# Attention units in turns of two, later ends of heads, and early output weights in a hybrid decoder layer

## The chip, the cores and the metric

The kernel runs on one core of a Trainium2 chip. The metric is the device time of one execution in microseconds (us); the lower, the better. The engines are named as in the profile: PE multiplies matrices (PEld loads its weights), DVE is the vector engine, ACT the activation engine, POOL the general one, SP issues most transfers. SBUF is the memory on the chip that all engines read, PSUM the eight banks into which PE writes its results.

## What is computed

One layer of a decoder for 1024 tokens of width 2048, in float32. The input is normalized, one projection (2048 to 6656 columns) gives eight groups, two kinds of attention follow, their outputs are normalized and gated, and an output projection (2048 by 2048) with another norm is added to the input. Cut to what matters here:

```python
q_sb, k_sb, v_sb, z_sb, q_sw, k_sw, v_sw, z_sw = split(einsum(rmsnorm(h), w_in))
# stick-breaking, 16 heads of 64, over all earlier keys
z = q_sb @ k_sb * scale
w = exp(log_sigmoid(z) + suffix_sum(log_sigmoid(-z)))      # only s < t
o_sb = w @ v_sb
# sliding window of 128, 16 heads on 4 key groups, with bias and a sink logit
p = softmax_with_sink(q_sw @ k_sw * scale + bias)
o_sw = p @ v_sw
o = concat(rmsnorm(o_sb) * silu(z_sb), rmsnorm(o_sw) * silu(z_sw))
h = h + rmsnorm(o @ w_out)
```

## The kernel before

**Projection.** The 6656 columns are 52 blocks of 128. A block is one call of `proj` (line 477): for each of 16 slices of the inner dimension and each of two halves of the tokens, three matmuls of 128x128 by 128x512 (high and low parts of both operands, since one float32r product is not exact enough). Weights come in four groups `kg` of four slices: `split_w` (line 128) loads a group into `wraw` by SP, ACT copies its high part (`whi`, line 133) and DVE subtracts the low part (`wlo`, line 135). After each slice and half, that is after every three matmuls, `step` (line 276) calls `advance`.

**Attention units.** Between those matmuls the attention is done in units, in the order in which `offer` queued them. A stick-breaking unit (`unit_sb`, line 535) is 256 rows by 256 keys of one head, 160 units in all, in 8 pairs of heads named sb0 to sb7; a unit sb3_0_1_2 is pair 3, head 0, row block 1, key block 2. A sliding-window unit (`unit_sw`, line 609) is 128 rows by 256 keys of two heads; there are 64, in groups sw0 to sw3. Each unit has three steps on PE, with work of other engines between them:

- `s1`: four score matmuls into `z` (PSUM tag pz, two banks). Then, for stick-breaking, two sigmoids on ACT (`m`, `b`: lines 555 and 557), two running products on DVE (lines 565, 568; a unit goes on from the `m` of the one before it in its row) and a product on DVE (line 571); on the diagonal a mask on POOL (line 561) comes before that. For the sliding window, a maximum, exponentials and a scaling on DVE and ACT (lines 639 to 654).
- `s2`: three or four transposes of the result into `wt` (PSUM tag pw, two banks); ACT copies the high part `wh`, DVE subtracts the low part `wl` (lines 586, 587 and 665, 666).
- `s3`: four output matmuls of `wh` and `wl` with the values `v` into `o` (PSUM tag po, **one** bank). Units of one row block of a stick-breaking head add up in the same `o`, which is copied to SBUF as `ot` by ACT after the last of them (`finish_o`, line 515); a sliding-window unit has an `o` of its own, copied after each unit. The next `o` can begin when that copy is done.

**The planner.** `advance` (line 152) sets the order on PE. It counts `pe_time`, its own estimate of PE's time, in which a 512-wide matmul is 0.213. A unit is begun when `period` has passed since the last (4.7 for stick-breaking, 3.8 for the sliding window) and fewer than `depth` (3) units wait between `s1` and `s2`; `s2` may follow `lag` (6.2 or 7.0) after `s1`, and `s3` follows `lag2` (4.5 or 5.0) after `s2`. Such a turn does the due `s3`, one `s2` and one `s1`, in that order. PE's order is kept as written; the other engines' lists are ordered by the scheduler of the framework, with the copies of `wh`, `wl`, `ot` and `v` preferred.

**Values and ends.** When the projection of the values of the next pair ends, `done_v_sb` (line 705) first drains what is left of the pair before (all steps at once, without regard to lags), then `evac_v` (line 407) scales the values on DVE and, 4.0 of `pe_time` later, transposes them on PE (`vt`) into the two `v` buffers.

**Background and output stage.** POOL adds pairs of output weights between the attention work (`sum_job`, line 243, tiles `bg` and `row_sw`, added at line 251), after their transfers have landed. At the end, the output projection is done as 7 products of half-size matrices (`mm_out`, line 930), each with 8 slices `e`, two column halves and four row blocks. `load_wo` and `split_wo` (lines 770, 781) bring its weight pieces in (`woraw`, then `wohi`, `wolo` on ACT and DVE). The first two are asked for after the last of the 52 blocks, zsb7, and the others during the output stage.

Of the kernel before, what the change touches and what calls it, by code (L numbers as in the profile page):

```python
# [19 lines left out]
P = 128  # L20
# [37 lines left out]
def layer(ctx, tc, xT, x, w_first, w_blk, w_out, g_pre, g_post, g_sb, g_sw, sinks, rel, onehot, penalty, out):  # L58
# [127 lines left out]
    def stage1_due(now):  # L186
        return 1 if stage1 and len(stage2) < 3 and stage1[0][0] + stage1[0][1]["lag"] <= now else 0

# [8 lines left out]
    def finish_stage1(force, now):  # L197
        if stage1 and len(stage2) < 3 and (force or stage1_due(now)):
# [208 lines left out]
    def evac_v(ps, name, lag=4.0):  # L407
# [69 lines left out]
    def proj(b, name, nxt=None, mid=None):  # L477
# [6 lines left out]
        for kg in range(4):  # L484
# [7 lines left out]
            for h in range(2):  # L492
                for j in range(4):
# [4 lines left out]
                    step()  # L498
        return ps
# [24 lines left out]
    def units_sb(pair, vst):  # L524
        units = []
        for hh in range(2):
            row = hh * HD
            head = {}
            for a in range(4):
                grp = {}  # L530
                for c in range(a, 4):
                    units.append(unit_sb(pair, hh, row, a, c, head, grp, vst[hh]))
        return units

    def unit_sb(pair, hh, row, a, c, head, grp, vs):
# [54 lines left out]
        def s3():  # L590
            if c == a:
                grp["o"] = po(f"o_{nm}")
            for j in range(2):
                for i, wt in enumerate(me["wt"]):
                    mm(grp["o"][:, :256], vs[:, 2 * c + j, :], wt[:, 2 - 2 * j:4 - 2 * j, :],
# [13 lines left out]
    def unit_sw(g, i, hp, head, vg):  # L609
# [59 lines left out]
        def s3():  # L669
            ops = po(f"o_{un}")  # L670
            for j in range(nj):
                for r, wt in enumerate(me["wt"]):
                    mm(ops[:, :256], vg[:, i + j, :], wt[:, j, :],
# [18 lines left out]
    def done_vsw(i):  # L692
        def f(ps):
            for g in range(2 * i):
                drain(f"sw{g}")
            vs["sw", 2 * i], vs["sw", 2 * i + 1] = evac_v(ps, f"vsw{i}", 4.0 if i else 9.0)
# [8 lines left out]
    def done_v_sb(p):  # L705
        def f(ps):
            for g in range(4):
                drain(f"sw{g}")
            drain(f"sb{p - 1}")
            offer(6.0, f"sb{p}", units_sb(p, evac_v(ps, f"vsb{p}")))  # L710
# [54 lines left out]
    RAW_TAGS = xtags[24:28]  # L765
    SPLIT_TAGS = xtags[28:32]
# [82 lines left out]
    for n, (b, name, done) in enumerate(work):  # L849
# [6 lines left out]
        if nxt is None:  # L856
            split_wo(2)
# [183 lines left out]
```

## Time and profile before

| what | value |
|---|---|
| median of 3 runs | 1794.3 us (1792.6 to 1796.31) |
| profiled execution | 1794.37 us |
| its span in the profile | 1792.5 us |
| mean granted PE clock | 0.998 |
| PE busy | 99% of the span, 9046 matmuls |
| DVE / ACT / POOL busy | 69% / 44% / 28% |
| traffic with main memory | 219.42 MB read, 91.23 MB written |

The span runs from the first instruction to the last; the execution's own time is 1.9 us longer. In rows of the timeline the columns are start in us, duration in us, engine, line, operation, output<-inputs, shape, count, and in brackets the idle time of the engine before it and what ended that. In rows of groups they are count, then busy us and mean ns of one, then idle time before them and its releasers. In rows of waits: who waited for whom, us in total, times, longest. Matmuls overlap in the pipeline, so PE's pace is read from the distance of starts, not from durations.

### The profile page before, as it was taken

The numbers are of one execution on the slowest core, as the hardware profiler recorded it, in microseconds if no ns is written. First come the engines' busy times: TensorE is split into PE (matmuls) and PEld (weight loads), VectorE is DVE, ScalarE is ACT, GpSimd is POOL, SyncE is SP. The second block draws the span as 40 slices with busy tenths as digits, with TensorE's granted clock in tenths as the row PEclk, the third lists the DMA queues.
The fourth block names the chain that finished last, engine by engine and source line by source line (L and its number), as shares of the span: only waits on it lengthen the run. The fifth ranks groups of instructions, "written<-read, shape, count | busy, mean of one in ns | idle before, by whom it ended". The sixth has DMA issues, their size and how long they took to land. (4 is left out here: it accounts for less than half of the span.)

```text
span 1792.5 us, 27351 instructions
## 1 busy us (share of the span) xinstructions
PE 1770.6 (99%) x9046; PEld 1500.1 (84%) x9046; DVE 1230.5 (69%) x1984; ACT 784.4 (44%) x1696; POOL 497.2 (28%) x648
## 2 busy tenths in 40 slices
PE   8999999999999999999999999999999999999998
PEld 7788888888888888888888888888888887888886
DVE  7567842678367688675785777767868646855795
ACT  7345531456344444343443444444434434444442
POOL 0012121211213334233233332232313224504533
PEclk9999999999999999999999999999999999999999
DMA  7557775566746656556456563454434385634484
GB/s 232 191 162 212 211 223 158 163 205 204 222 134 182 181 168 190 162 182 183 156 166 178 177 181 124 154 164 142 146 106 136 103 256 190 210 100 140 136 286 155
DMA packets 203884, 312.48 MB, mean 174 GB/s; under 512 B 24640, under 2 KB 84192, under 8 KB 203616
## 3 DMA queue, kind: packets, MB, share of 16 engines
q1 hardware_dynamic: 201680, 307.60, 55.8%
q10 hardware_dynamic: 2064, 3.15, 0.5%
q8 instruction: 72, 1.18, 0.3%
q14 instruction: 68, 0.56, 0.1%
HBM read 219.42 MB, written 91.23 MB: 173 GB/s over the span
## 5 line engine op out<-in xcount | busy, mean ns | idle before, releaser
L587 DVE TENSOR_TENSOR wl_sb<-wt_sb,wh_sb 128x512 fp32r<-128x512 f32 (+1 forms) x160 | 100.7, 633 | 95.8 <-ACT wh_sb L586 95.8
L571 DVE TENSOR_TENSOR b_sb<-b_sb,m_sb 128x512 f32<-128x512 f32 x160 | 129.2, 807 | 42.1 <-POOL b_sb L561 19.1
L586 ACT CAST wh_sb<-wt_sb 128x512 fp32r<-128x512 f32 (+1 forms) x160 | 87.0, 544 | 136.3 <-PE wt_sb L126 134.3
L568 DVE TENSOR_TENSOR_SCAN m_sb<-m_sb,m_sb,zero 128x257 f32<-128x257 f32 x192 | 143.4, 785 | 2.4 <-ACT m_sb L555 2.1
L933 PE MATMUL y<-wohi,x 128*128 128x512 f32 x448 | 141.9, 393 | 1.5 <-ACT wohi L797 1.5
L933 PE MATMUL y<-wohl,x 128*128 128x512 f32 x576 | 132.5, 389 | 0.0
L933 PEld LDWEIGHTS y<-wohl,x 128*128 128x128 f32 x576 | 108.1, 188 | 22.4
L565 DVE TENSOR_TENSOR_SCAN m_sb<-m_sb,mask 128x256 f32<-128x256 f32 x128 | 119.8, 972 | 5.8 <-ACT m_sb L555 5.8
L648 ACT ACTIVATE L_sw<-L_sw,nm_sw 128x256 f32<-128x256 f32 (+1 forms) x128 | 63.1, 494 | 93.1 <-DVE nm_sw L643 91.7
L122 PE MATMUL p_vsb<-xh,whi_vsb 128*128 128x512 f32 x256 | 102.0, 398 | 0.0
L933 PEld LDWEIGHTS y<-wohi,x 128*128 128x128 f32 x448 | 84.9, 189 | 19.9 <-ACT wohi L797 1.9
L122 PE MATMUL p_ksb<-xh,wlo_ksb 128*128 128x512 f32 x256 | 100.7, 393 | 0.0
L122 PE MATMUL p_qsb<-xh,whi_qsb 128*128 128x512 f32 x256 | 100.6, 393 | 0.0
L122 PE MATMUL p_zsw<-xh,wlo_zsw 128*128 128x512 f32 x256 | 100.6, 393 | 0.0
L122 PE MATMUL p_qsb<-xh,wlo_qsb 128*128 128x512 f32 x256 | 100.6, 393 | 0.0
L122 PE MATMUL p_vsb<-xh,wlo_vsb 128*128 128x512 f32 x256 | 100.5, 393 | 0.0
L122 PE MATMUL p_ksb<-xl,whi_ksb 128*128 128x512 f32 x256 | 100.5, 392 | 0.0
L122 PE MATMUL p_vsb<-xl,whi_vsb 128*128 128x512 f32 x256 | 100.4, 392 | 0.0
L122 PE MATMUL p_qsb<-xl,whi_qsb 128*128 128x512 f32 x256 | 100.4, 392 | 0.0
L122 PE MATMUL p_zsw<-xl,whi_zsw 128*128 128x512 f32 x256 | 100.4, 392 | 0.0
L122 PE MATMUL p_zsb<-xh,wlo_zsb 128*128 128x512 f32 x256 | 100.4, 392 | 0.0
L122 PE MATMUL p_zsb<-xl,whi_zsb 128*128 128x512 f32 x256 | 100.2, 391 | 0.0
(243 smaller groups left out, 4988.3 us busy)
## 6 DMA issues: line engine op xcount, KB each, us to landing
row_sw<-in_w_out SPq DMA_DIRECT2D x80, 256.0 KB, 4.3
bg<-in_w_out SPq DMA_DIRECT2D x80, 256.0 KB, 4.3
woraw<-wsum SPq DMA_DIRECT2D x80, 256.0 KB, 3.4
kh<-kd SPq DMA_DIRECT2D x160, 64.0 KB, 2.9
kl<-kd SPq DMA_DIRECT2D x160, 64.0 KB, 2.4
wsum<-row_sw SPq DMA_DIRECT2D x40, 256.0 KB, 2.9
wsum<-bg SPq DMA_DIRECT2D x40, 256.0 KB, 3.3
q_sw<-qd SPq DMA_DIRECT2D x64, 128.0 KB, 3.5
```

The costliest lines, as they stand in the source:

```text
L122: tc.keep_in_program_order(nc.tensor.matmul(ps, a, b, start=start, stop=stop))
L565: nc.vector.tensor_tensor_scan(m[:, tb, 1:257], m[:, tb, 1:257], mask[:, P - P * tb:P - P * tb + 256], m[:, tb, 0:1], ALU.mult, ALU.max)
L568: nc.vector.tensor_tensor_scan(m[:, tb, :], m[:, tb, :], zero.to_broadcast([P, 257]), prev[:, tb, 256:257], ALU.mult, ALU.max)
L571: nc.vector.tensor_mul(beta, beta, m[:, :, 0:256])
L586: nc.scalar.copy(wh[:, :k], pt[:, :k])
L587: nc.vector.tensor_sub(wl[:, :k], pt[:, :k], wh[:, :k].bitcast(F32))
L648: nc.scalar.activation(L[:, hh, :n], L[:, hh, :n], AF.Exp, bias=nm[:, hh:hh + 1], accum_out=sm[:, hh:hh + 1])
L933: nc.tensor.matmul(ps, xt[:, a, tcols], w[b][:, cols], start=first and n == 0, stop=last and n == 2)
```

## The change

It has three parts.

1. A turn now comes every two periods and handles two units: first one due `s3`, then up to two due `s2`, then up to two `s1`, then all other due `s3`. The test against `depth` in `advance` goes (`start` still holds it at 3).
2. The drain of the pair before moves from the end of the values' projection to the moment when the new values are transposed, 4.0 of `pe_time` later, and goes by `s3`, `s2`, `s1` directly. The `v` tiles are taken at that moment, so units get the list `vst` and look the tile up in `s3`.
3. The first eight pieces of output weights are loaded in the middle of the last block zsb7 (`early_last`), into the tiles of slices 0 to 3 of the input, which that block has read by then. They are split, one after every three matmuls, in its last quarter, into the tiles of slices 4 to 7.

```diff
@@ advance
-        if len(stage1) - stage1_due(now) < todo[0]["depth"] and last_start[0] + todo[0]["period"] <= now:
+        if last_start[0] + 2 * todo[0]["period"] <= now:
+            finish_stage2(False, now)
+            turned = finish_stage1(False, now) and finish_stage1(False, now)
+            begun = start(now) and (not todo or start(now))
             while finish_stage2(False, now):
                 pass
-            late = len(stage1) >= todo[0]["depth"]
-            if late:
-                finish_stage1(False, now)
-            begun = start(now)
-            if not late:
-                finish_stage1(False, now)
-            return begun
+            return begun or turned
@@ drain
-            assert advance(True)
+            assert finish_stage2(True, pe_time[0]) or finish_stage1(True, pe_time[0]) or start(pe_time[0])
@@ evac_v
-        vst = [at.tile([P, 8, P], F32R, tag="v", name=f"v_{name}_{j}") for j in range(2)]
+        vst = []
         us = [scaled(ps[h], name, h) for h in range(2)]
         def finish(h):
+            if h == 0:
+                for key in ended:
+                    drain(key)
+                vst.extend(at.tile([P, 8, P], F32R, tag="v", name=f"v_{name}_{j}") for j in range(2))
@@ proj
                     step()
+                    if kg == 3 and nxt is None:
+                        split_wo(4 * h + j + 1)
@@ done_v_sb
-            for g in range(4):
-                drain(f"sw{g}")
-            drain(f"sb{p - 1}")
-            offer(6.0, f"sb{p}", units_sb(p, evac_v(ps, f"vsb{p}")))
+            ended = [f"sw{g}" for g in range(4)] + [f"sb{p - 1}"]
+            offer(6.0, f"sb{p}", units_sb(p, evac_v(ps, f"vsb{p}", ended)))
@@ mids
+    def early_last():
+        load_wo(8)
+        early(f"zsb{NPAIR - 1}", NPAIR - 1)()
+
+    mids[f"zsb{NPAIR - 1}"] = early_last
@@ load_wo
-            if k < 8 or k % 7 < 3:
+            if k < 8:
+                raw = xp.tile([P, HALF], F32, tag=EARLY_TAGS[k], name=f"woraw{k}")
+            elif k % 7 < 3:
@@ split_wo
+            elif k < 8:
+                t = xp.tile([P, 2, HALF], F32R, tag=EARLY_TAGS[8 + k], name=f"wohl{k}")
+                hi, lo = t[:, 0, :], t[:, 1, :]
             else:
-                alt = k % 8 // 2 if k >= 8 else 0
+                alt = k % 8 // 2
@@ main loop
-        if nxt is None:
-            split_wo(2)
```

Three places show what this does to the lists of the engines. The first is PE in the middle of a stick-breaking head (pair 3, head 0). Names are those of the tiles: `o` output, `wt` transposes, `z` scores, `p` projection; the last number is a serial one. Before, a turn between two stretches of the projection:

```order
L122 MATMUL p_ksb4_1_9508<-xh4_269,wlo_ksb4_1_9513 128x512
L122 MATMUL o_sb3_0_0_9521<-wh_sb3_0_0_2_9531,v_vsb3_0_9227 128x256
L122 MATMUL o_sb3_0_0_9521<-wl_sb3_0_0_2_9532,v_vsb3_0_9227 128x256
...
L126 MATMUL wt_sb3_0_1_1_9619<-ident_190,b_sb3_0_1_1_9467 128x128 x3
L122 MATMUL z_sb3_0_2_2_9629<-kh_1065,q_sb3_0_2_9474 128x256
L122 MATMUL z_sb3_0_2_2_9629<-kl_1066,q_sb3_0_2_9474 128x256
...
L122 MATMUL p_ksb4_1_9508<-xh5_300,whi_ksb4_1_9511 128x512
```

And after, from the same output on:

```order
L122 MATMUL p_ksb4_1_9485<-xh5_300,wlo_ksb4_1_9490 128x512
L122 MATMUL o_sb3_0_0_9501<-wh_sb3_0_0_2_9511,v_vsb3_0_9255 128x256
...
L126 MATMUL wt_sb3_0_1_1_9604<-ident_190,b_sb3_0_1_1_9531 128x128 x3
L126 MATMUL wt_sb3_0_1_2_9614<-ident_190,b_sb3_0_1_2_9548 128x128 x4
L122 MATMUL z_sb3_0_1_3_9623<-kh_1065,q_sb3_0_0_9285 128x256
...
L122 MATMUL z_sb3_0_2_2_9636<-kh_1065,q_sb3_0_2_9538 128x256
...
L122 MATMUL o_sb3_0_0_9501<-wh_sb3_0_0_3_9520,v_vsb3_0_9255 128x256
L122 MATMUL o_sb3_0_0_9501<-wl_sb3_0_0_3_9521,v_vsb3_0_9255 128x256
...
L122 MATMUL p_ksb4_1_9485<-xh6_336,whi_ksb4_1_9488 128x512
```

One turn has taken the place of two; in the whole list the projection resumes 203 times after other work instead of 324, and 33 of its matmuls stand between two turns of a stick-breaking head where there were 15 or 18. The two units whose transposes stand in this turn had their scores in the turn before; before the change, two more turns lay between. Both outputs here go to one row block, so to one `o`.

The second place is PE in the sliding window (group 0, its units 4 to 7). Before, twelve matmuls of the projection stand between the turns of the two outputs:

```order
L122 MATMUL o_sw0_5_0_1577<-wh_sw0_5_0_1480,v_vsw0_0_832 128x256
L122 MATMUL o_sw0_5_0_1577<-wl_sw0_5_0_1481,v_vsw0_0_832 128x256
...
L126 MATMUL wt_sw0_7_0_1585<-ident_190,L_sw0_7_0_1431 128x128 x2
L122 MATMUL z_sw0_2_1_1592<-kh_1065,q_sw0_2_1_1446 128x256
...
L122 MATMUL p_qsw3_1_1299<-xh8_408,whi_qsw3_2_1451 128x512
...
L122 MATMUL o_sw0_6_0_1626<-wh_sw0_6_0_1532,v_vsw0_0_832 128x256
L122 MATMUL o_sw0_6_0_1626<-wl_sw0_6_0_1533,v_vsw0_0_832 128x256
```

After the change:

```order
L122 MATMUL o_sw0_4_0_1607<-wh_sw0_4_0_1453,v_vsw0_0_915 128x256
...
L126 MATMUL wt_sw0_7_0_1615<-ident_190,L_sw0_7_0_1462 128x128 x2
L122 MATMUL z_sw0_2_1_1622<-kh_1065,q_sw0_2_1_1477 128x256
...
L122 MATMUL o_sw0_5_0_1642<-wh_sw0_5_0_1513,v_vsw0_0_915 128x256
L122 MATMUL o_sw0_5_0_1642<-wl_sw0_5_0_1514,v_vsw0_0_915 128x256
...
L122 MATMUL o_sw0_6_0_1650<-wh_sw0_6_0_1522,v_vsw0_0_915 128x256
L122 MATMUL o_sw0_6_0_1650<-wl_sw0_6_0_1523,v_vsw0_0_915 128x256
...
L122 MATMUL p_qsw3_1_1279<-xh14_643,whi_qsw3_3_1492 128x512
```

Three outputs of three units, each with an `o` of its own, now stand in one turn, two of them side by side. In this stage turns with three outputs alternate with turns that have none: 30 matmuls of the projection stand before each of the former and 9 or 12 before each of the latter. Such a pair of outputs of different `o` side by side stands 16 times in the sliding window and once at the end of sb7.

The third place is the list of transfers on SP around the last weights of the last block. Before:

```order
L131 DMA wraw_zsb7_3_15543<-in_w_blk 128x512
...
L815 DMA xs0_7_15585<-ogs7_123 128x512
L778 DMA woraw0_15611<-wsum0_0_132 128x512
L815 DMA xs1_0_15876<-w21_0_124 128x512
L778 DMA woraw1_15613<-wsum0_1_133 128x512
L434 DMA or_zsb7_0_15539<-od7_90 64x2x512 x2
```

After:

```order
L131 DMA wraw_zsb7_3_15559<-in_w_blk 128x512
...
L785 DMA woraw0_15539<-wsum0_0_132 128x512
...
L785 DMA woraw7_15553<-wsum0_7_139 128x512
L432 DMA or_zsb7_0_15555<-od7_90 64x2x512 x2
...
L825 DMA xs0_7_15601<-ogs7_123 128x512
```

Eight pieces `woraw` follow the last weights of the block, ahead of the last input tile of the output stage (`xs0_7`) and of the gate's operand (`or_zsb7_0`).

More of the change, by code (lines that the diff above doesn't have):

```diff
@@ L184, in start @@
         return True
-    def stage1_due(now):
-        return 1 if stage1 and len(stage2) < 3 and stage1[0][0] + stage1[0][1]["lag"] <= now else 0
     def finish_stage2(force, now):
@@ L197, in finish_stage1 @@
     def finish_stage1(force, now):
-        if stage1 and len(stage2) < 3 and (force or stage1_due(now)):
+        if stage1 and len(stage2) < 3 and (force or stage1[0][0] + stage1[0][1]["lag"] <= now):
             u = stage1.pop(0)[1]
@@ L531, in units_sb, with unit_sb @@
                 for c in range(a, 4):
-                    units.append(unit_sb(pair, hh, row, a, c, head, grp, vst[hh]))
+                    units.append(unit_sb(pair, hh, row, a, c, head, grp, vst))
         return units
-    def unit_sb(pair, hh, row, a, c, head, grp, vs):
+    def unit_sb(pair, hh, row, a, c, head, grp, vst):
         nm = f"sb{pair}_{hh}_{a}"
@@ L594, in s3 @@
                 for i, wt in enumerate(me["wt"]):
-                    mm(grp["o"][:, :256], vs[:, 2 * c + j, :], wt[:, 2 - 2 * j:4 - 2 * j, :],
+                    mm(grp["o"][:, :256], vst[hh][:, 2 * c + j, :], wt[:, 2 - 2 * j:4 - 2 * j, :],
                        start=(c == a and j == 0 and i == 0), stop=(c == 3 and j == 1 and i == 1))
@@ L672, in s3 @@
                 for r, wt in enumerate(me["wt"]):
-                    mm(ops[:, :256], vg[:, i + j, :], wt[:, j, :],
+                    mm(ops[:, :256], vg()[:, i + j, :], wt[:, j, :],
                        start=(j == 0 and r == 0), stop=(j == nj - 1 and r == 1))
@@ L693, in f @@
         def f(ps):
-            for g in range(2 * i):
-                drain(f"sw{g}")
-            vs["sw", 2 * i], vs["sw", 2 * i + 1] = evac_v(ps, f"vsw{i}", 4.0 if i else 9.0)
+            vst = evac_v(ps, f"vsw{i}", [f"sw{g}" for g in range(2 * i)], 4.0 if i else 9.0)
+            for j in range(2):
+                vs["sw", 2 * i + j] = lambda j=j: vst[j]
         return f
@@ L765, in layer @@
     RAW_TAGS = xtags[24:28]
+    EARLY_TAGS = xtags[0:16]
     SPLIT_TAGS = xtags[28:32]
```

3 lines of the change are left out of this document (1 added, 2 removed).

## The prediction

> **What bounds the kernel now.** I read the page first, its span and busy times, then PE's waits, then PE's timeline where waits or slow stretches show.
>
> ```profile
> span 1792.5 us, 27351 instructions
> PE 1770.6 (99%) x9046; PEld 1500.1 (84%) x9046; DVE 1230.5 (69%) x1984; ACT 784.4 (44%) x1696; POOL 497.2 (28%) x648
> ```
>
> PE is busy all the time, so only three things can shorten the run: waits of PE, slower pace of PE, or less work; the change takes no work away. The waits of PE, all that the profile has:
>
> ```profile
> PE f0a L122 <- ACT whi_f L332: 5.8, 1, 5.8
> PE o_sb L122 <- ACT ot_sb L518: 3.1, 3, 1.4
> PE wt_sb L126 <- DVE wl_sb L587: 1.6, 1, 1.6
> PE y L933 <- ACT wohi L797: 1.5, 1, 1.5
> PE o_sw L122 <- ACT ot_sw L518: 1.3, 4, 0.5
> PE y L933 <- DVE wolo L798: 0.3, 1, 0.3
> ```
>
> The first is the start of the kernel, which is not touched. The other five come to 7.8 us. More than that, 0.4% of the run, can't be won from waits. The rest of a gain has to come from pace.
>
> **Part 1, fewer turns: -4.0 us.** Here is the projection after one turn (scores, then projection) up to the next turn; the rows are the first, the tenth and the nineteenth after the scores.
>
> ```profile
> 509.14 0.40 PE L122 MATMUL p_zsw<-xh,whi_zsw 128*128 128x512 f32 x1
> ...
> 511.22 0.39 PE L122 MATMUL p_zsw<-xh,whi_zsw 128*128 128x512 f32 x1
> ...
> 513.26 0.49 PE L126 MATMUL wt_sb<-ident,b_sb 128*128 128x128 f32 x3
> ```
>
> The first nine matmuls take 2.08 us, the next nine 2.04: a turn costs 0.04 us of pace in what follows it. Counted in PE's list, stretches of nine or more projection matmuls after other work go from 236 to 147, shorter ones from 88 to 56. 89 x 0.04 = 3.6 and 32 x 0.013 (a third of it for three matmuls) = 0.4. The number of small matmuls stays, so this is all there is: 4.0 us, surely between 3 and 5.
>
> **Part 3, early output weights: -3.9 us.** PE's timeline where the output stage begins:
>
> ```profile
> 1478.37 0.39 PE L933 MATMUL y<-wohi,x 128*128 128x512 f32 x1
> ...
> 1480.23 0.50 PE L933 MATMUL y<-wohi,x 128*128 128x512 f32 x1 [1.48 <-ACT wohi L797]
> ...
> 1481.04 0.50 PE L933 MATMUL y<-wolo,x 128*128 128x512 f32 x1 [0.30 <-DVE wolo L798]
> ...
> 1483.11 1.06 PE L933 MATMUL y<-wohi,x 128*128 128x512 f32 x2
> ...
> 1486.18 0.39 PE L933 MATMUL y<-wolo,x 128*128 128x512 f32 x1
> ```
>
> From 1478.37 to 1486.18 there are 17 matmuls. At the calm 0.227 (2.04 / 9) they take 3.86; they took 7.81. So 3.9 us are lost here: 1.8 in two waits for a piece of weight, the rest at 0.43 each, when PE's clock had been lowered:
>
> ```profile
> 836.00:839.00 3.00, 1.39 (x9) 0.96 (x8) 2.36 (x4) 0.48 (x1) 0.35 (x3) 1.00 0.60 194
> ...
> 1480.00:1486.00 6.00, 5.46 (x16) 4.15 (x17) 3.26 (x6) 2.27 (x5) 2.56 (x2) 0.72 0.60 196
> ```
>
> (The columns are the stretch and its length, busy PE, PEld, DVE, ACT, POOL, then the granted clock, DMA share and GB/s.) The granted clock was 0.72 there, but 1.00 around the wait of 1.6 us at 837.9. With eight pieces split in the last block both waits go and with them the slow stretch. What it adds: eight transfers behind the block's last weights in SP's list, and one split per three matmuls in the last quarter, where no attention is left; ACT and DVE have 0.62 and 0.69 for it within 3 x 0.227 = 0.68. What could be late next is xs0_7, which SP now issues behind those eight, but it is needed only for the eighth slice, some 19 us into the stage. I take the whole 3.9; the low end is 1.8, if the clock drops anyway.
>
> The Trainium skill ("TensorE: Matmul & The Clock Gate", section "Part 1: The HAM clock gate") says that PE falls to half its clock only after an idle window of about 3.4 us. Taken alone it would not put the slow stretch down to waits of 1.5 and 0.3 us, and would leave 1.8 us to win instead of 3.9. The trace shows pace 0.43 right behind them, so the measurement decides, and I keep 3.9.
>
> **Part 1 again, outputs side by side: +12.1 us.** There is one bank for `o`. A sliding-window unit's next output has to wait until ACT has copied the last one. The rows show a copy that comes at once, one that comes late, and one for which PE waits:
>
> ```profile
> 165.79 0.28 PE L122 MATMUL o_sw<-wl_sw,v_vsw 128*128 128x256 f32 x1
> ...
> 166.16 0.37 ACT L518 COPY ot_sw<-o_sw 128x256 f32<-128x256 f32 x1
> ...
> 191.00 0.28 PE L122 MATMUL o_sw<-wl_sw,v_vsw 128*128 128x256 f32 x1
> ...
> 193.83 0.35 ACT L518 COPY ot_sw<-o_sw 128x256 f32<-128x256 f32 x1
> ...
> 198.91 0.35 ACT L518 COPY ot_sw<-o_sw 128x256 f32<-128x256 f32 x1
> ...
> 199.32 0.39 PE L122 MATMUL o_sw<-wh_sw,v_vsw 128*128 128x256 f32 x1 [0.22 <-ACT ot_sw L518]
> ...
> 199.54 0.28 PE L122 MATMUL o_sw<-wl_sw,v_vsw 128*128 128x256 f32 x1
> ...
> 199.77 0.28 PE L122 MATMUL o_sw<-wl_sw,v_vsw 128*128 128x256 f32 x1
> ...
> 199.89 0.60 PE L126 MATMUL wt_sw<-ident,L_sw 128*128 128x128 f32 x4
> ...
> 200.80 0.39 PE L122 MATMUL p_qsb<-xh,whi_qsb 128*128 128x512 f32 x1
> ```
>
> After the start of an output's last matmul: 0.28 to its end, 0.09 until the copy starts (165.79 + 0.28 = 166.07, 166.16), 0.35 for it, 0.06 until PE goes on (199.26, 199.32). That is 0.78, less 0.12 that the next matmul would need anyway, and 0.05 to 0.10 more because the first two matmuls after a wait stand 0.22 apart. With the copy starting 0.04 after its matmuls, as it does at best, it is 0.71 in all. Before, the projection's 12 matmuls, 2.7 us, covered this. Side by side nothing covers it: 17 x 0.71 = 12.1 us. ACT free is the best case; the least I can make of it is 0.55 each, 9.4.
>
> **The first output of a turn and the second: +3 us.** Between them stand four transposes and four scores. From 199.77 to 200.80 that is 1.03 us, against the 0.73 to 0.78 needed, so a copy that starts up to 0.3 late is covered. In 16 such turns of the sliding window a copy like that of 193.83, which started 2.55 after its matmuls because ACT's list has exponentials waiting for DVE ahead of it, would stop PE for 2.2. Over the 64 copies of the timeline the delay goes from 0.04 to 3.5 with a mean of 0.9, and what exceeds 0.3 is 0.67 on average: 16 x 0.67 = 10.7 at most. At least it is nothing: the turns with outputs now come after 30 matmuls, 6.8 us after the last scores, where it was 2.7, so DVE has mostly caught up. I take a quarter, near the row of 166.16. The 1.3 us of such waits in PE's list above are gone with the old order: **-1.3**.
>
> One more wait is new. A turn's third copy finds both `ot` buffers taken, and needs the transfer of the first to have landed:
>
> ```profile
> DMA to landing us min/median/max: 1.8/3.1/5.1
> ```
>
> That is 3.1 us after its issue, while the third copy is wanted some 2 us after the first. It stops ACT for 1 to 2 us, with the exponentials of the turn's new scores behind it, and DVE's scaling behind those. I cost it at nothing, since the transposes that need these come after 9 to 12 more projection matmuls and, for the turn's own unit, a whole turn later; if a fifth of the 1.5 still came through in each of the 16 turns, it would be 5 us, which goes into the high end.
>
> **Stick-breaking, less room for DVE: +3 us.** Rows of DVE between 600 and 1290 us, and what DVE waited for over the run:
>
> ```profile
> L568 DVE TENSOR_TENSOR_SCAN m_sb<-m_sb,m_sb,zero 128x257 f32<-128x257 f32 x142 | 107.4, 794 | 1.9 <-ACT m_sb L555 1.6
> L571 DVE TENSOR_TENSOR b_sb<-b_sb,m_sb 128x512 f32<-128x512 f32 x118 | 94.9, 804 | 33.1 <-POOL b_sb L561 13.5 <-POOL m_sb L559 9.5 <-ACT whi_zsb L133 0.5
> ...
> L587 DVE TENSOR_TENSOR wl_sb<-wt_sb,wh_sb 128x512 fp32r<-128x512 f32 x70 | 48.1, 687 | 38.2 <-ACT wh_sb L586 38.2
> ...
> L135 DVE TENSOR_TENSOR wlo_vsb<-wraw_vsb,whi_vsb 128x512 fp32r<-128x512 f32 x23 | 17.6, 766 | 0.8 <-ACT whi_vsb L133 0.6
> ...
> L390 DVE TENSOR_TENSOR u_vsb<-p_vsb,rstd 128x512 f32<-128x512 f32 x12 | 8.2, 687 | 22.8 <-PE p_vsb L122 18.1 <-DMA od<-ot_sb 2.5 <-DMA w<-bg 2.1
> ```
>
> ```profile
> DVE b_sb L571 <- POOL b_sb L561: 19.1, 8, 4.3
> ...
> DVE b_sb L571 <- POOL m_sb L559: 9.5, 3, 3.4
> ```
>
> A turn of two units is 33 x 0.227 = 7.5 of projection and 24 small matmuls, twice the 1.38 of 199.32 to 200.80 without its 0.10: 10.3 us. DVE has two units, each 0.687 + 2 x 0.794 + 0.804 = 3.1, then 33 / 24 of a weight split of 0.77 and a third of a block's two scalings of 0.69: 7.7 us. About 0.75 goes by from the transposes until DVE can begin. So some 1.8 us of room are left, and the chains end in time in an ordinary turn. Before, a unit's transposes came three turns, some 14 us, after its scores. What uses the room up are the 11 waits for POOL, whose list has background additions waiting for transfers ahead of masks; they are 28.6 us, 2.6 each. Past 1.8 that is 0.8 x 11 = 9 us of new waits, against 4.7 (3.1 and 1.6 in PE's list) paid today for the same lateness. I take +3 instead of the 4.3, as some of the 11 fall on turns that have more room than an ordinary one; the ends are -4.7 (all gone) and +12 (each late by one more us).
>
> Part 2 gets no price of its own. In PE's list the last outputs of each pair stand ahead of the new values' transposes with projection between them, before the change and after, so that the drain finds nothing to do; only at the end of sb7 it sets two outputs side by side, which is the seventeenth above. The values' own steps on DVE and ACT stay behind the same transposes. If a drain had to force a unit, the price would be one chain of 7.7 / 2 and the steps around it, some 5 us; the list shows none.
>
> **The sum.** -4.0 - 3.9 - 1.3 + 12.1 + 3 + 3 = +8.9 us on the profiled execution's 1794.4 (span 1792.5 and 1.9 around it; the median is 1794.3): **1803 us**. A measurement of this kernel can tell about 0.2%, 3.6 us, from no change.
>
> **The rivals.**
> - *The late copies and late masks don't come* (both +3 at their low ends): -9.2 + 12.1 + 0 - 2 = +1, 1795 us, no change that can be measured. For it: 6.8 us for DVE to catch up. Chance 0.18.
> - *Faster*: outputs side by side cost little, because the copy overlaps or the pairs are fewer in effect, about 0.2 us each: -9.2 + 3.4 - 2 = -8, 1786 us. It decides below 0.4 us each. Against it stands the row of 199.32, where PE went on 0.06 after the copy, so that one really holds it. Chance 0.12.
> - *The score chains are late in every stick-breaking turn*: DVE's room of 1.8 is eaten by waits for ACT and POOL, and each of 80 turns loses 0.4: 32 in place of my 3, 1832. Against it: the sum of 7.7 in 10.3. Chance 0.10.
> - *The waits lower the clock*: if waits of 0.7 twice in a turn do what 1.5 and 0.3 did at 1480, each of 16 turns costs nine matmuls 0.2 more, +29: 1832. Against it the 1.00 around the longer single wait at 837.9. Chance 0.05. By the rule of the Trainium skill named above ("TensorE: Matmul & The Clock Gate", the same section) it could not happen, as no window of 3.4 us would be idle.
>
> My forecast (1798 to 1812) has the other 0.55.
>
> **The range.** Low ends: -4.5 - 3.9 - 1.3 + 9.4 + 0 - 4.7 = -5.0, 1789; high ends: -3 - 1.8 - 1.3 + 13 + 10.7 + 5 + 12 = +35, 1829. Eight in ten lie between 1787 and 1818. Faster 0.12, same 0.18, slower 0.70.
>
> **What would show it.** PE's waits should list `o_sw <- ot_sw` with some 12 to 20 us in over 20 times, 0.6 to 0.7 each; the rows of `y <- wohi` and `wolo` should be gone and the clock 1.00 in the first 10 us of the output stage; the first nine matmuls after a turn should still take 0.04 more. I am wrong if waits for `ot_sw` stay under 5 us, or if waits for `wl_sb`, `b_sb` or `z_sb` come to more than 10 us.

## The result and the profile after

The changed kernel takes 1812.8 us (median of 5, 1810.65 to 1815.52) against 1794.3 (1792.04 to 1796.31): 1.0106 times as long, 95% interval 1.0093 to 1.012. That is 18.5 us slower, where 8.9 was forecast. The profiled execution took 1815.24, its span is 1813.5, 21.0 longer than before. The page of the changed kernel, and PE's waits:

```profile
span 1813.5 us, 27295 instructions
PE 1776.9 (98%) x9046; PEld 1503.6 (83%) x9046; DVE 1239.3 (68%) x1984; ACT 774.8 (43%) x1696; POOL 509.7 (28%) x648
```

```profile
PE o_sw L122 <- ACT ot_sw L518: 12.9, 21, 2.3
PE f0a L122 <- ACT whi_f L326: 5.8, 1, 5.8
PE p_vsb L122 <- DVE wlo_vsb L135: 3.4, 2, 3.2
PE o_sb L122 <- ACT ot_sb L518: 2.0, 2, 1.4
PE wt_sb L126 <- DVE b_sb L571: 2.0, 2, 1.5
PE p_zsw L122 <- DVE u_ksb L384: 1.2, 1, 1.2
PE p_zsb L122 <- DVE wlo_zsb L135: 0.6, 2, 0.4
PE o_sb L122 <- POOL m_sb L559: 0.2, 1, 0.2
```

Without the start these are 22.3 us; before they were 7.8. The waits of `y` are gone, the waits of `o_sw` went from 1.3 to 12.9, and there are waits of the projection itself (`p_vsb`, `p_zsw`, `p_zsb`), of which there were none.

Where along the program the time went is read from matmuls ahead of which the same work has been done in both kernels. The first gate matmul `p_zsw` and the first output matmul `y` are such marks. In PE's timeline, first of before, then of after:

```profile
495.87 0.39 PE L122 MATMUL p_zsw<-xh,whi_zsw 128*128 128x512 f32 x1
...
1473.16 0.39 PE L933 MATMUL y<-wohi,x 128*128 128x512 f32 x1
```

```profile
514.11 0.39 PE L122 MATMUL p_zsw<-xh,whi_zsw 128*128 128x512 f32 x1
...
1498.18 9.00 PE L941 MATMUL y<-wohl,x 128*128 128x512 f32 x39
```

Part A (the span's start to `p_zsw`, with all of the sliding window) went from 495.9 to 514.1, +18.2. Part B (to `y`, with nearly all of stick-breaking) went from 977.3 to 984.1, +6.8. Part C (the output stage) went from 319.3 to 315.3, -4.0. The sum is the span's +21.0. The forecast's terms, sorted by these parts, were about +12.3, +0.5 and -3.9 (A: 16 pairs 11.4, late copies 3, old waits -1.3, 32 short stretches fewer -0.4 and some of the long ones -0.4; B: one pair 0.7, room 3, 80 turns fewer -3.2). So part C is as forecast, and both A and B cost some 6 us more.

**In the output stage** the 9.00 us of 39 matmuls above come to 0.23 each. The windows of the changed kernel (columns as before: the sixth number after the length is the granted clock) show a clock of 1.00 there (last row), and two places where the clock fell instead (second and third row). The 0.86 of the third is a mean over a stretch that begins before the fall; from 618.6 to 621.8 the clock was 0.50 as well.

```profile
195.00:200.00 5.00, 4.15 (x25) 3.52 (x26) 4.81 (x11) 1.77 (x6) 1.10 (x1) 1.00 0.50 160
253.60:259.00 5.40, 4.90 (x17) 4.11 (x18) 2.44 (x7) 2.36 (x8) 0.00 (x0) 0.50 0.51 110
614.80:620.00 5.20, 1.98 (x6) 1.34 (x5) 4.72 (x6) 0.33 (x1) 1.74 (x2) 0.86 0.34 110
1498.00:1508.00 10.00, 10.00 (x46) 8.29 (x45) 7.66 (x12) 5.83 (x11) 2.59 (x2) 1.00 0.85 272
```

**Outputs side by side** in the timeline (PE's rows, then ACT's, of an ordinary turn of the sliding window):

```profile
166.61 0.28 PE L122 MATMUL o_sw<-wl_sw,v_vsw 128*128 128x256 f32 x1
167.35 0.39 PE L122 MATMUL o_sw<-wh_sw,v_vsw 128*128 128x256 f32 x1 [0.46 <-ACT ot_sw L518]
167.58 0.28 PE L122 MATMUL o_sw<-wl_sw,v_vsw 128*128 128x256 f32 x1
...
166.93 0.37 ACT L518 COPY ot_sw<-o_sw 128x256 f32<-128x256 f32 x1 [0.37 <-PE o_sw L122]
```

From 166.61 to 167.35 are 0.74 where 0.12 would do, and the next matmul follows after 0.23: 0.62 + 0.11 = 0.73 each, as forecast (0.71).

**A late copy**, which was not. ACT's and PE's rows some 20 us later, with one of DVE's:

```profile
185.39 0.37 ACT L518 COPY ot_sw<-o_sw 128x256 f32<-128x256 f32 x1 [4.28 <-DMA od<-ot_sw]
...
186.88 0.16 DVE L651 TENSOR_TENSOR sm_sw<-sm_sw,es_sw 128x2 f32<-128x2 f32 x1 [3.22 <-ACT es_sw L650]
...
191.78 0.51 ACT L648 ACTIVATE L_sw<-L_sw,nm_sw 128x256 f32<-128x256 f32 x1
...
193.88 0.49 ACT L648 ACTIVATE L_sw<-L_sw,nm_sw 128x256 f32<-128x256 f32 x1
...
194.97 0.36 ACT L518 COPY ot_sw<-o_sw 128x256 f32<-128x256 f32 x1
...
195.38 0.38 PE L122 MATMUL o_sw<-wh_sw,v_vsw 128*128 128x256 f32 x1 [1.57 <-ACT ot_sw L518]
```

At 185.39 a third copy has stopped ACT for 4.28 us, until the transfer of the first had freed its buffer. The exponentials behind it are late by that, and DVE waits 3.22 us for them with its own list behind. So the exponentials of the next two units are late in turn: from 191.78 to 194.4 they stand ahead of the next turn's first copy, and PE waits 1.57 us for it. (In e5 below, which has a third buffer, the same exponentials run from 189.08 to 191.8, and PE does not wait.) ACT's list has 41.6 us of such stops in all, in 15 copies:

```profile
ACT ot_sw L518 <- DMA od<-ot_sw: 41.6, 15, 5.1
```

**The longest wait** is in part B (rows of POOL, DVE, PE):

```profile
611.25 1.28 POOL L434 TENSOR_TENSOR or_zsw<-or_zsw 128x512 f32<-128x512 f32 x1 [9.46 <-DMA or_zsw<-od]
...
612.56 1.16 DVE L449 TENSOR_TENSOR u_zsw<-u_zsw,or_zsw 128x512 f32<-128x512 f32 x1 [2.74 <-POOL m_sb L559]
...
613.14 1.73 POOL L245 TENSOR_TENSOR bg<-bg 128x512 f32<-128x512 f32 x1
613.64 1.78 DVE L571 TENSOR_TENSOR b_sb<-b_sb,m_sb 128x512 f32<-128x512 f32 x1
615.34 2.39 DVE L565 TENSOR_TENSOR_SCAN m_sb<-m_sb,mask 128x256 f32<-128x256 f32 x2
617.65 0.66 DVE L135 TENSOR_TENSOR wlo_vsb<-wraw_vsb,whi_vsb 128x512 fp32r<-128x512 f32 x1
...
618.37 0.69 PE L122 MATMUL p_vsb<-xh,wlo_vsb 128*128 128x512 f32 x1 [3.22 <-DVE wlo_vsb L135]
```

POOL waits for a transfer of earlier outputs until 611.25; the gate multiplication on DVE (L449) waits for that sum, the chain steps of two units stand behind it, and behind them the split of the weights that the projection needs next. The page names the memset that POOL does last (`m_sb`); what DVE needs is `or_zsw`, which ends just before it. One more thing makes this wait long: the product `b_sb` takes 1.78 us here, beside a background addition on POOL, against a mean of 0.80 before.

### The profile page after: what moved, and what is told of

Read it like the earlier page. It is cut to its first block, busy times and chain, and to the rows that moved or that the text cites. A ratio compares the mean times of both kernels' runs of the same rounds, so it can differ in the third digit from the quotient of the medians.

```text
span 1813.5 us, 27295 instructions
## 1 busy us (share of the span) xinstructions
PE 1776.9 (98%) x9046; PEld 1503.6 (83%) x9046; DVE 1239.3 (68%) x1984; ACT 774.8 (43%) x1696; POOL 509.7 (28%) x648
## 5 line engine op out<-in xcount | busy, mean ns | idle before, releaser
L587 DVE TENSOR_TENSOR wl_sb<-wt_sb,wh_sb 128x512 fp32r<-128x512 f32 (+1 forms) x160 | 97.0, 634 | 129.1 <-ACT wh_sb L586 128.7
L941 PE MATMUL y<-wohl,x 128*128 128x512 f32 x672 | 155.0, 390 | 0.0
L941 PEld LDWEIGHTS y<-wohl,x 128*128 128x128 f32 x672 | 126.2, 188 | 26.6 <-issue 0.5
L586 ACT CAST wh_sb<-wt_sb 128x512 fp32r<-128x512 f32 (+1 forms) x160 | 81.6, 546 | 152.8 <-PE wt_sb L126 151.9
L565 DVE TENSOR_TENSOR_SCAN m_sb<-m_sb,mask 128x256 f32<-128x256 f32 x128 | 126.6, 1018 | 5.9 <-POOL m_sb L559 4.1
L941 PE MATMUL y<-wohi,x 128*128 128x512 f32 x384 | 120.2, 389 | 0.0
L122 PE MATMUL p_zsw<-xh,whi_zsw 128*128 128x512 f32 x256 | 100.1, 391 | 1.2 <-DVE u_ksb L384 1.2
L122 PE MATMUL p_ksb<-xh,whi_ksb 128*128 128x512 f32 x256 | 100.5, 393 | 0.0
L122 PE MATMUL p_zsb<-xh,whi_zsb 128*128 128x512 f32 x256 | 100.0, 390 | 0.0
```

The lines of the kernel that those rows point to most:

```text
L122: tc.keep_in_program_order(nc.tensor.matmul(ps, a, b, start=start, stop=stop))
L565: nc.vector.tensor_tensor_scan(m[:, tb, 1:257], m[:, tb, 1:257], mask[:, P - P * tb:P - P * tb + 256], m[:, tb, 0:1], ALU.mult, ALU.max)
L586: nc.scalar.copy(wh[:, :k], pt[:, :k])
L587: nc.vector.tensor_sub(wl[:, :k], pt[:, :k], wh[:, :k].bitcast(F32))
L941: nc.tensor.matmul(ps, xt[:, a, tcols], w[b][:, cols], start=first and n == 0, stop=last and n == 2)
```

## The experiments

Two theories stood for part A: the bank of `o` alone (0.7 in each of 16 pairs), or ScalarE's lists and buffers. For part B: additions on POOL that wait for transfers, or too little room on DVE. All times are medians of several runs beside runs of the kernel before (1793.7 to 1794.6 in the four groups); A and B are read from each kernel's trace as above.

| kernel | turns of two in | time | ratio to before, 95% | A | B |
|---|---|---|---|---|---|
| before | none | 1794.3 | | 495.9 | 977.3 |
| after | both | 1812.8 | 1.0093 to 1.012 | 514.1 | 984.1 |
| e1 | none | 1791.1 | 0.9981 to 1.0 | 497.4 | 975.6 |
| e2 | stick-breaking | 1798.8 | 1.0013 to 1.0034 | 496.1 | 985.5 |
| e3 | sliding window | 1806.2 | 1.0052 to 1.008 | 509.5 | 983.8 |
| e4 | both | 1804.9 | 1.0049 to 1.0074 | 506.5 | 983.5 |
| e5 | both | 1805.2 | 1.0037 to 1.007 | 504.5 | 984.2 |
| e6 | both | 1794.5 | 0.9986 to 1.0008 | 495.1 | 980.6 |
| e7 | stick-breaking | 1909.6 | 1.0617 to 1.0661 | 496.9 | 1089.7 |
| e8 | stick-breaking | 1796.8 | 1.0 to 1.0018 | 497.8 | 980.5 |
| e9 | sliding window | 1793.9 | 0.9992 to 1.0012 | 496.9 | 978.6 |
| e10 | none | 1791.4 | 0.9974 to 1.0004 | 497.5 | 978.0 |
| e11 | both | 1821.8 | 1.0136 to 1.0168 | 497.2 | 1001.8 |
| e12 | sliding window | 1799.2 | 1.0019 to 1.0039 | 498.1 | 979.9 |
| f1 | both | 1785.6 | 0.9935 to 0.9966 | 493.0 | 975.5 |
| f2 | sliding window | 1782.5 | 0.992 to 0.9948 | 493.7 | 971.5 |
| f3 | none | 1803.3 | 1.0038 to 1.0076 | 498.0 | 988.1 |
| f4 | both | 1796.8 | 0.9999 to 1.0021 | 497.5 | 982.4 |

Except in e7, e11 and e12, the span after `y` is 315.2 to 315.6 in every kernel with early output weights, against 319.3 before.

**e1, e2, e3: which part of the change costs.** In `advance`, for e2 (e3 with the two names exchanged, e1 with the old rule alone):

```diff
+        if todo[0]["key"].startswith("sb"):
             if last_start[0] + 2 * todo[0]["period"] <= now:
...
+        else:
+            if len(stage1) - stage1_due(now) < todo[0]["depth"] and last_start[0] + todo[0]["period"] <= now:
...
```

e1: 

> The changed kernel with the old rule for turns everywhere; the later ends and the early output weights stay. Theory (the three parts add up, and only the turns cost): the kernel before less the 4.1 us that the start of the output stage gained, 1790.2. Rival (later ends put the new values' steps in the way, or the eight early loads delay the last block): 1794 or more.

e2: 

> The changed kernel with the old rule for the sliding window's turns only; stick-breaking keeps turns of two. Theory: the 18.2 us lost by the first gate projection (time at which its first matmul starts, 495.9 before, 514.1 after) go away, the 6.8 of the stick-breaking stage stay: 1794.6. Forecast's own terms (stick-breaking +3 - 2.7): 1790.7. Rival (the stick-breaking waits are left over from the sliding window's lateness): 1788 to 1790.

e3: 

> The changed kernel with the old rule for stick-breaking's turns only; the sliding window keeps turns of two. Theory: the sliding window's 18.2 us stay and stick-breaking's 6.8 go: 1806. Rival (both stages' losses are one, handed on): 1800 or less, or 1812 as now.

e1 and e3 came out as their theories said, e2 4 us above its own. Parts 2 and 3 alone are worth 3.1 us (1794.25 to 1791.1, at the edge of the noise, as the interval reaches 1.0; the output stage is 4.0 shorter in the trace): the early weights pay and the later ends cost nothing that shows. Against e1, turns of two cost 7.7 us in stick-breaking alone and 15.1 in the sliding window alone, together 22.8; the changed kernel stands 21.7 above e1. But A and B show that e3's 15.1 isn't the sliding window's alone: its A is 12.1 above e1's, and its B 8.2, although B has the old turns (its profiled execution, 1810.3, was the slowest of its five, so that A and B together are 5 too long against e1). Its list of waits has this row in B, where e1's has 2.4 for the same, and the clock was 0.50 around both of these waits:

```profile
PE wt_sb L126 <- DVE wl_sb L602: 7.7, 2, 4.0
```

So part B can lose several us in either order; what it loses has to be compared with care (f1, f2 below).

**e4, e5, e6: bank and buffers.** e4 writes an output that stands behind another at a turn's end into a bank of the scores; e5 keeps the bank and gives the copies three buffers; e6 does both.

```diff
-            while finish_stage2(False, now):
-                pass
+            while finish_stage2(False, now, spare):
+                spare = True
...
-            ops = po(f"o_{un}")
+            ops = (pz if spare else po)(f"o_{un}")
```

```diff
-        ot = at.tile([P, 256], F32, tag="ot", name=f"ot_{name}")
+        ot = at.tile([P, 256], F32, tag="m", name=f"ot_{name}", bufs=3) if row is None else at.tile([P, 256], F32, tag="ot", name=f"ot_{name}")
```

e4: 

> The changed kernel, but an output that stands right behind another in a sliding-window turn is written to a bank of the scores, which is free then; TensorE's order is the same. Theory (one bank handed over side by side costs 0.85 us in each of 16 turns): 13.6 less, 1799. Rival (the copies are late by what ScalarE and VectorE have to do, so the wait only moves to the next turn): 1808 or more.

e5: 

> The changed kernel with three buffers instead of two for the copied outputs of the sliding window (in tiles that stick-breaking uses later). Theory (the third copy's wait for its buffer holds ScalarE, but no matmul): 1812 to 1813, no change, TensorE's waits for the copies still 11 us or more. Rival (ScalarE's waits for buffers, 41.6 us in the list of the changed kernel, are what makes the first copies late): 1807 or less.

e6: 

> The kernel of e4 with three buffers for the copied outputs. Theory (in e4 the third copy came 1 to 2 us later because both buffers were taken, and the scores that use that bank next waited 4.1 us for it): these 4.1 go, 1800.8. Rival (the copy is late because of the exponentials ahead of it): 1804 or more, waits of the scores as in e4.

e4 took 7.9 off, between theory and rival. In its list the waits have moved in part to the scores that use that bank next, since the third copy still has no buffer:

```profile
PE o_sw L122 <- ACT ot_sw L519: 5.1, 4, 1.9
PE z_sw L122 <- ACT ot_sw L519: 4.1, 5, 1.5
```

e5 took 7.6 off, against my theory: the third buffer is not free of charge. What is left of its waits is the pairs and nothing else, 16 times 0.46:

```profile
PE o_sw L122 <- ACT ot_sw L518: 7.4, 16, 0.5
```

e6 took 18.4 off, 6 more than its theory said and 10.8 more than e5. That is 0.67 for each of 16 pairs (by the traces, A is 9.4 shorter than in e5, although e6 has 2.1 of other waits for copies there). Its A of 495.1 is as short as before the change, so bank and buffers are the whole loss of the sliding window. It takes another bank, not the free half of this one. The Trainium skill ("PSUM — Partial Sum Buffer", section "PSUM bank collisions raise a hardware error ⚠️") says that TensorE may not write to a bank while another engine reads any part of it in the same quadrant. No run here tried it; the rows above only show that PE goes on right after the copy.

**e7, e8: late additions and gates.** e7 gives a background addition more time after its loads, e8 puts the gate multiplication of the second half later:

```diff
             BG(nc.sync.dma_start(t[:, 1, :], w_view(b, e, cols)))
-            yield 8.0
+            yield 13.0
```

```diff
-            defer(12.0, lambda: gate(1, o1))
+            defer(17.0, lambda: gate(1, o1))
```

e7: 

> The kernel of e2 (turns of two in stick-breaking alone), with the background additions of output weights put 13 instead of 8 units of planned time after their loads are issued. TensorE's order is the same. Theory (each larger wait of stick-breaking is an addition on GpSimd that still waits for its transfer, with masks and squares queued behind it): the wait of 2.9 us for a copied output and the slow clock after it go, that of 3.4 for a piece of weight stays (its addition is not one of the background): 3 to 5 us less, 1794 to 1796. Rival (units in pairs leave VectorE too little room by themselves): 1798 to 1800 as e2, other waits in place of these.

e8: 

> The kernel of e2, with each second gate multiplication put 17 instead of 12 units of planned time after its block. Theory (VectorE stood before this multiplication for a transfer with the next units' chain and a weight split behind it): the wait of 3.4 us for a piece of weight goes, with 0.8 of slow clock; 1793 to 1796. Rival (no room on VectorE): 1798 to 1800 as e2.

The place that e7 is about, in e2 (POOL, ACT and PE):

```profile
1084.38 1.28 POOL L260 TENSOR_TENSOR bg<-bg 128x512 f32<-128x512 f32 x1 [9.19 <-DMA bg<-in_w_out]
1085.62 1.26 POOL L449 TENSOR_TENSOR or_zsb<-or_zsb 128x512 f32<-128x512 f32 x1
...
1086.91 0.63 ACT L467 ACTIVATE acc_sb<-or_zsb 128x512 f32<-128x512 f32 x1 [6.30 <-POOL m_sb L574]
1087.45 0.35 ACT L533 COPY ot_sb<-o_sb 128x256 f32<-128x256 f32 x1
...
1087.94 0.55 PE L122 MATMUL o_sb<-wh_sb,v_vsb 128*128 128x256 f32 x1 [2.93 <-ACT ot_sb L533]
```

In e7 this wait is gone and the program is 4.8 us ahead of e2 after it, up to the last block. Its time says nothing, though: with longer jobs the additions were not through when the output stage began, which shows as one wait:

```profile
PE y L956 <- ACT x L849: 107.9, 1, 107.9
```

In e8 the wait of 3.4 for a piece of weight is gone (its list still has 0.2 for `p_vsb`, at another place), and the clock stays at 1.00 there. B fell by 5.0, although new waits of 3.2 for `b_sb` came (five, at most 0.9). The median, 1796.8, fell by only 2.1 and lies between theory and rival; A, whose order is that of e2, happens to be 1.7 longer in this trace. So the wait that ends at 618.4 in the changed kernel hangs on that gate, and part of what its move wins comes back.

**e9 to e12: what the parts are worth together.** e9 is e6 with the old turns in stick-breaking, e10 is e1 with three copy buffers, e11 and e12 are e6 and e9 with both moves of e7 and e8, at 10 instead of 13.

e9: 

> The kernel of e6 (other bank, three copies) with the old rule for stick-breaking's turns: turns of two in the sliding window alone, with what they lacked. Theory (the losses of the two stages add up; stick-breaking's was 7.7 by e2 less e1): 1794.5 - 7.7 = 1786.8, faster than both kernels. Rival (part of e6's gain only replaces waits of stick-breaking): 1790 or more.

e10: 

> The kernel of e1 (old turns everywhere) with three copy buffers as in e5. Theory (with an output per turn and 12 projection matmuls between, the third buffer is hardly missed): 1789.5 to 1791. Rival (the third buffer, and not the turns of two, is what e9 wins by): the same time as e9, 1787.

e11: 

> The kernel of e6 with both moves of e7 and e8, the background additions at 10 instead of 13 so that they end in time. Theory (stick-breaking's loss is made of a few additions and multiplications that wait for transfers with other steps behind them): 5 less than e6, 1789 to 1790. Rival (VectorE's room): 1793 or more, as e6.

e12: 

> The kernel of e9 with the same two moves. Theory: stick-breaking's old turns had 4.7 us of such waits in the kernel before, of which half goes: 1784. Rival (with a unit per turn the chains have room for late additions): as e9.

e9 missed by 7: it is no faster than e6. In its A, turns of two with bank and buffers are as good as the old turns (496.9 and 497.4), and in B it met a wait of 2.8 us for `wl_sb`, with the slow clock after it. e10 equals e1, as expected: with one output per turn the third buffer is not missed. e11 and e12 missed as e7 did: `y` waited 22.5 us in e11, and e12's output stage is 320.3 long.

**f1 to f4: additions left out, and shifted.** f1 and f2 are e6 and e9 without the addition itself (its loads and stores stay), f3 and f4 are e1 and e6 with the addition 11 after the loads and the store 3 after it, so that a job is no longer.

```diff
-            BG((nc.gpsimd.tensor_add if sign > 0 else nc.gpsimd.tensor_sub)(t[:, 0, :], t[:, 0, :], t[:, 1, :]))
             yield 6.0
```

f1: 

> The kernel of e6 (turns of two everywhere, other bank, three copies) without the background additions of output weights on GpSimd; their loads and stores stay. Left out: the sums of output weights, so the output is another. Orders on TensorE, ScalarE and VectorE are unchanged. Theory (stick-breaking loses where an addition waits for its transfer ahead of other GpSimd steps): the stick-breaking stage falls from 980.6 to 976 or less, 1790 or less. Rival (VectorE has too little room): 979 or more in that stage, 1793 or more.

f2: 

> The kernel of e9 (turns of two in the sliding window alone, freed) without the same additions, which are left out as in f1. Theory: the old turns have such waits too (2.8 and 1.7 us in e9's trace), the stage falls from 978.6 to about 975, 1790, and f1 is within 1.5 of it. Rival (room): f1 is slower than this by 3 or more.

f3: 

> The kernel of e1 with each background addition 11 instead of 8 units after its loads and its store 3 instead of 6 after it, so that a job is no longer than before. Theory: most additions find their operands there; its stick-breaking stage falls from 975.6 to 974 or less, 1788 to 1790, which would be the fastest of all. Rival (the store, waiting on the queue for an addition 3 units before it, makes the transfers behind it late): 1792 or more.

f4: 

> The kernel of e6 with the same shift. Theory (late additions make the loss): 2 to 4 less than e6, 1790 to 1792. Rival (room): 1794 or more.

The additions cost 8.9 us in e6 and 11.4 in e9. f1 came out as its theory said; f2 is 7.5 below the 1790 expected, and 3.1 below f1 where 1.5 was expected. PE's waits without them, of f1 and of f2 (the rows after the start):

```profile
PE p_vsb L122 <- DVE wlo_vsb L135: 2.2, 2, 2.0
PE o_sw L122 <- ACT ot_sw L518: 0.9, 1, 0.9
PE wt_sb L126 <- DVE b_sb L571: 0.9, 1, 0.9
PE o_sb L122 <- ACT ot_sb L518: 0.6, 1, 0.6
PE p_zsb L122 <- DVE wlo_zsb L135: 0.3, 1, 0.3
```

```profile
PE o_sw L122 <- ACT ot_sw L533: 0.6, 1, 0.6
```

With the old turns stick-breaking has no wait at all then. With turns of two it has 2.2 + 0.9 + 0.6 + 0.3 = 4.0, and B is 975.5 against 971.5, the same 4.0; the times differ by 3.1. So neither theory holds alone: turns of two cost 3 to 4 us of room by themselves (half of it, 2.0, behind the gate of e8, for which DVE still stands 2.5 us in f1), and the rest is additions, which cost either order.

How the additions cost is only in part what f1's theory says. Here is part B of e6, then of f1, with the same 960 instructions on DVE (third pair of numbers):

```profile
495.10:1475.70 980.60, 972.33 (x5190) 832.32 (x5189) 696.23 (x960) 414.95 (x815) 303.98 (x490) 1.00 0.55 163
493.00:1468.50 975.50, 971.37 (x5189) 832.45 (x5188) 674.15 (x960) 414.68 (x815) 233.52 (x441) 1.00 0.55 163
```

DVE's waits for POOL in B hardly differ (14.4 us in e6, 15.1 in f1), but DVE's own instructions take 22 us less when no addition runs beside them. With the old turns, from e9 to f2, both fall: the waits from 30.9 to 11.0, the busy time from 703.9 to 685.1. So an addition costs in two ways, by what stands behind it on POOL and by what runs beside it on DVE. No run here separates the two.

f3 and f4 were slower than what they came from, by 12.1 and 2.3, as their rivals said: moving the additions moves what they collide with. In f3's trace PE's waits in B are 13.5 us, against 3.3 in e1. The longest is 3.75 us, for a copy behind a stop of ACT that waits 6.96 us for the store `wsum<-row_sw` (2.49 at the same place in e1), and the clock is 0.50 for 3.3 us after it.

No kernel that computes everything is clearly faster than before; e1, at 1791.1, comes closest.

## Why the prediction was off

The direction was right and the size was half: 1812.8 lies inside the wide range (1787 to 1818), but just above the forecast's own 1798 to 1812. By its own steps:

- **Fewer turns, -4.0.** The effect is there, the gain hardly. Summed over all first nine projection matmuls after other work, what exceeds 0.2265 each fell from 10.2 us to 5.6 (single ones over 0.26 left out). But take a stretch nearly without waits, from a first `p_ksb` to a first `p_vsb` matmul; in e2 it has 18 stretches of projection fewer than in e1, 14 of them long. The marks in e1, then in e2:

```profile
874.75 0.39 PE L122 MATMUL p_ksb<-xh,whi_ksb 128*128 128x512 f32 x1
...
1050.74 0.39 PE L122 MATMUL p_vsb<-xh,whi_vsb 128*128 128x512 f32 x1
```

```profile
875.11 0.39 PE L122 MATMUL p_ksb<-xh,whi_ksb 128*128 128x512 f32 x1
...
1050.93 0.39 PE L122 MATMUL p_vsb<-xh,whi_vsb 128*128 128x512 f32 x1
```

  They are 175.99 and 175.82 apart: 0.17 us won, where 14 x 0.04 + 4 x 0.013 = 0.6 was due. "The number of small matmuls stays, so this is all there is" was the mistake, and this step failed: by their starts the projection's matmuls take 0.78 us less in this stretch, but the small ones 0.62 more. All of B says the same. In the kernels whose clock stayed at 1.00 in B, B less PE's waits is 972.5 (before), 972.3 (e1) and 971.5 (f2) with the old turns, and 972.6 (e6), 972.4 (e8) and 971.6 (f1) with turns of two. Of the 3.2 us that were counted on there, nothing shows.
- **Early output weights, -3.9.** Right: C fell by 4.0, and the clock was 1.00 there. With the later ends, which I priced at nothing, it is 3.1 in e1's time.
- **Outputs side by side, +12.1.** Right in mechanism and size: 10.8 for 16 by e5 against e6, and one pair of 0.61 at the end of sb7 as foreseen.
- **First output of a turn and the second, +3, and the third copy, nothing.** This step failed. I found the third copy's wait for its buffer, with the exponentials behind it, and wrote "I cost it at nothing". The cover I named, 9 to 12 projection matmuls, is some 2.7 us, and ACT was stopped for up to 5.1. It came through as late first copies (waits of 1.57, 2.34, 0.75 and less) and as a slow clock (0.50 from 253.4 to 260.0): e5, in which nothing is changed but the third buffer, is 7.6 us faster, and there the first and second output of a turn cost 0.1. The +3 and the 0 were one term of 7.6 (10.4 once the pairs have their bank, from e4 to e6), and the 5 that I had put into the high end was too low as well.
- **Stick-breaking, less room for DVE, +3.** Right in its working, too low in what was taken. Of the terms for B, 0.5 in all, came 6.8. Half of the difference is the pace above. PE's waits in B went from 4.7 to 9.4 (the list of after without the start and `o_sw`), which is 4.7 more where +3 and 0.7 for the one pair stood. The slow clock behind the wait of 3.22 had no price; it cost 1.6, by the spacing of the matmuls from 618.4 to 621.8. That the step "0.8 x 11 = 9 us of new waits, against 4.7" came so near to 9.4 is partly luck: I looked for the waits at the units' own transposes, and the largest stood at a weight split of the projection, which shares DVE's list. That POOL's list with its transfers stops DVE was named rightly, and e7 and e8 show it at two places. That DVE's own instructions are longer beside POOL's additions has no term in the prediction. Over the kernels whose DVE and POOL work is unchanged, B is 977.3, 975.6, 978.0, 978.6 and 983.8 with the old turns, and 984.1, 985.5, 983.5, 984.2 and 980.6 with turns of two, on average 4.9 apart, and a single wait with the slow clock behind it moves one kernel by as much (these are single executions).
- **The rivals.** The two without a loss that can be measured fell with the pairs' 0.67. "The waits lower the clock" happened twice, with single waits of 2.34 and 3.22 us, but never after a pair's 0.46. The sign of being wrong, more than 10 us of waits for "`wl_sb`, `b_sb` or `z_sb`", asked for the wrong names: those came to 2.0, so the chains were not late in every turn either.

That e6 lost 3.6 us less in B than e5, with the same stick-breaking, is mostly the clock. At the same matmul PE waits 3.31 us in e5 and 3.10 in e6, and then (e5, e6; the number before the last two is the clock):

```profile
608.50:615.00 6.50, 5.69 (x22) 5.31 (x23) 3.11 (x6) 1.45 (x3) 0.45 (x3) 0.50 0.47 128
598.00:604.50 6.50, 5.38 (x35) 4.89 (x36) 4.87 (x9) 2.94 (x6) 0.42 (x4) 1.00 0.42 119
```

What stays open is at which places additions and units meet in a given order, and why the clock falls behind one such wait and not behind another.

## What to carry to other kernels

When steps are put together in pairs, count each thing that one of them holds until another engine or a transfer is done (banks, copy buffers), and give the pair as many as it takes; a stop on an engine's list is paid by whoever stands behind it, even if its own result is not urgent. A wait that is hidden today is hidden by the distance between steps, so before that distance is shortened, look for the transfers that other engines wait for, not only for the engine's sum of work. And compare parts of the program between marks with the same work done, since single waits of 3 us at chance places, with or without a slow clock behind them, hide a difference of 5 in the total; take both off before two paces are compared.

## What the hardware showed

- PE's clock fell to 0.50 around idle times below 3.4 us, and not around every one. In the changed kernel it was 0.50 from 253.4 to 260.0, around a wait of 2.34 us that ended at 253.6, and from 618.6 to 621.8, behind one of 3.22, with a matmul of 0.69 in place of 0.39; in e4 it was 0.50 from 168.2 to 171.4, behind one of 1.93. After 1.57 and 0.46 at 195 it stayed at 1.00, and in e8 from 1074 to 1080 too, around a wait of 3.39. So in these runs the length of a wait alone does not decide. The Trainium skill ("TensorE: Matmul & The Clock Gate", section "Part 1: The HAM clock gate (the "warmup" mystery)") speaks of an idle window of about 3.4 us; in these runs less was enough.
- Transposes and scores in runs of eight are no faster than in runs of four: in the stretches of 175.99 and 175.82 above, by their starts, the 116 transposes take 1.39 us more and the 128 scores 1.06 less.
- DVE's instructions took longer beside additions on POOL: 696.2 us for the 960 of part B in e6, 674.2 without the additions in f1. Of the 160 products `b_sb` in e6, the 112 that run beside no POOL instruction of more than 0.5 us take at most 0.70 us each, the others up to 2.88.
